# A hybrid decoder step: the second mixer's scores two steps sooner, its values turned later, and one function table loaded two steps later

## The chip, the cores and the metric

The kernel runs on one core of one Trainium2 chip. The metric is device time in microseconds (us). Engines: TensorE (PE) multiplies matrices, VectorE (DVE) and ScalarE (ACT) work on elements, GpSimd (POOL) gathers and moves, SyncE (SP) issues most transfers. All share one on-chip memory; matmul results go to a separate memory of a few buffers, which DVE and ACT read. Each engine runs its own instructions in the order in which the program gives them, and waits by semaphores for the others.

## What is computed

One layer of a decoder step for a prompt of 512 positions and 8 samples of one position each (520 columns in all), with a width of 2048. Two mixers work side by side on the same normed input: an mLSTM (matrix memory) and FoX (forgetting attention, 8 heads of 128). Their outputs are merged by gates, projected, and followed by a gated feed-forward part with a short convolution. The part of the reference that matters here is the prompt's attention and the merge:

```python
def block(args):
    qi, Fi, i = args
    qpos = i * Q_BLOCK + jnp.arange(Q_BLOCK)
    s = jnp.einsum('bqhd,bkhd->bhqk', qi, k).astype(jnp.float32) * scale
    s = s + (Fi.transpose(0, 2, 1)[..., :, None] - FkT[:, :, None, :])
    s = jnp.where(qpos[:, None] >= kpos[None, :], s, -jnp.inf)
    p = jax.nn.softmax(s, axis=-1).astype(v.dtype)
    return jnp.einsum('bhqk,bkhd->bqhd', p, v)
...
merged = jax.nn.sigmoid(ga) * (y_m @ w_proj_a) + jax.nn.sigmoid(gb) * (y_f @ w_proj_b)
x = x + g1 * (merged @ w_out)
```

Numbers are 32-bit floats. A product is made of three matmuls of rounded parts (high by high, high by low, low by high): ACT rounds a tile to its high part (`CAST`), DVE subtracts to get the low part (names that end in h and l).

## The kernel before

The kernel goes through the stages in order: conditioning and norms, the mLSTM, the input projections, the second mixer (FoX), the projections and merge, the output projection, the feed-forward part. In nearly all of them PE multiplies weights that stream in from memory, and the other engines prepare the next weights beside it.

**The second mixer.** Its attention alone would leave PE waiting for DVE and ACT, so it is woven into 16 half-products of the last 8 gates: 128 steps, each with six matmuls of the gate (`gate`, 260 columns each), 8 steps to a half. The loop is at the end of the listing below: behind a step's matmuls come the casts and loads of coming gate weights at fixed steps (`gate_cast` on ACT, `gate_low` on DVE, `gate_load` on SP), and then the pieces that `plan` holds for this step. `put(s, f, H)` enters a piece. Pieces of one step run in the order in which they were entered: all heads first, in order, then the samples' pieces (`s_*`). Each engine gets its instructions in just this order.

A head starts every `HP` = 13 steps at b = 1 + 13 * head. A head lasts 25 steps, so two are under way at any time. Its pieces:

- `f_load`, `f_roots`: SP loads q, k, the reciprocal roots of their norms (`rq`, `rk`, from `drr`) and V (from `dv`), all into tiles named `fi`. `f_norm`: two DVE instructions scale q and k.
- `f_forget`: a matmul spreads the head's forget sums (`nFb`), ACT copies them (`nfb`). `f_split`, `f_split_low`: high and low parts of q and k (`fqh`, `fkh` on ACT, `fql`, `fkl` on DVE).
- `f_values`: four transposes turn V (`vtp`), ACT makes its high part and copies the last block (`fvh`, `last`); `f_values_low`: `fvl` on DVE.
- `f_scores` i (0 to 3): block i of 128 queries against the (i+1)*128 keys up to it, into `fS`, with the mask added by one more matmul. `f_max` i: DVE adds the forget sums and finds the minimum in one custom instruction (`fs`, `sm`), ACT takes the exponential and its row sum. `f_scale` i: DVE divides (reciprocal, `fs<-fs,sm`).
- `f_turn` j (0 to 2): transposes the scaled rows of key block j, 4, 4 and 2 transposes, into `fPT`; block 3 is done beside block 1. ACT makes `fph`. `f_turn_low`: DVE makes `fpl` from `fPT` and `fph`.
- `f_attend` j: the product with V into `fy`; `f_result`: ACT copies it out.

Tiles of the matmul memory for these pieces (`nFb`, `vtp`, `fS`, `fPT`, `fy`, and the samples' `sS`, `sPT`, `sO`) come from one pool of four buffers, `pm`, handed out in turn: a new tile waits until the last reader of the tile four back is done with it.

Up to step 70 DVE also works off the sample scores (`s_scores`: a product `raw<-raw,qb` and a sum `sc<-raw`, two pieces for each i). Steps 71 to 81 hold the samples' softmax: `s_turn` (74, `sS`), `s_max`, `s_scale` (78, on DVE, tile `pp`), `s_weights` (79, transposes `sPT` of `pp`); then come the gathered values (`sO`).

**The output projection** runs in `run_pairs`: 7 products to a unit, and `late` gives functions to run ahead of the product of one step. At step 9 stands `log_exp`, which has ACT load the table that holds the logarithm and the exponential for the norm behind this stage. The products of a unit go to the tiles `x` and `y`; ACT copies `x` to `tg` before PE may write `x` again.

Of the kernel before, what the change touches and what calls it, by code (L numbers as in the profile page):

```python
# [18 lines left out]
P = 128  # L19
# [4 lines left out]
N = SEQ + NS  # L24
# [39 lines left out]
def tile_hybrid_step(ctx: ExitStack, tc: tile.TileContext, I, O):  # L64
    nc = tc.nc
    S, V, G, T, Y = nc.scalar, nc.vector, nc.gpsimd, nc.tensor, nc.sync
# [13 lines left out]
    def nm(s):  # L80
        uid[0] += 1
        return f"{s}{uid[0]}"
# [4 lines left out]
    def mconst(shape, name, dt=F32, tag=None):  # L87
        return cm.tile(shape, dt, tag=tag or name, name=name)

    def st(name, dt=F32):  # L90
        return sp.tile([P, 528], dt, tag="s", name=nm(name))
# [13 lines left out]
    def dram(shape, name):  # L105
        return dp.tile(shape, F32, tag=nm(name), name=nm(name))
# [68 lines left out]
    def on(f, *a):  # L175
        return lambda: f(*a)
# [550 lines left out]
    for i, (c0, n) in enumerate(phases):  # L727
        todo = {j: [] for j in range(NPRE)}

        def put(j, f, *a):  # L730
            todo[j].append(on(f, *a))
# [13 lines left out]
        if i + 1 < len(phases):  # L745
            a, b = range(c0 + n, c0 + 2 * n)
# [113 lines left out]
    for e in range(2):  # L860
        t = mconst([P, NS * NPG], f"idxf{e}")
# [355 lines left out]
    H = mheads = follows = None  # L1217
# [95 lines left out]
    dv = dram([FH, P, N], "dv")  # L1313
# [163 lines left out]
    dss, drr = dram([2, FH, N], "dss"), dram([2, FH, N], "drr")  # L1477
# [4 lines left out]
            Y.dma_start(t[:, :N], src)  # L1482

    def f_roots(H):
        H.rq, H.rk, H.v = st("fi"), st("fi"), st("fi")
        for t, src in ((H.rq, drr[0, H.i].partition_broadcast(P)), (H.rk, drr[1, H.i].partition_broadcast(P)),
                       (H.v, dv[H.i])):
            Y.dma_start(t[:, :N], src)

    def f_norm(H):  # L1490
        for t, w, r in ((H.q, qwc, H.rq), (H.k, nkw, H.rk)):
            V.scalar_tensor_tensor(t[:, :N], t[:, :N], w, r[:, :N], op0=ALU.mult, op1=ALU.mult)
        H.rq = H.rk = None
# [5 lines left out]
    for hh in range(FH):  # L1499
        H = Head()  # L1500
        H.i, H.p, H.pt, H.fs, H.sm, H.tp = hh, [], {}, {}, {}, {}
        heads.append(H)
    H = None
# [80 lines left out]
    for j in range(KC):  # L1584
# [11 lines left out]
        if j < NG:  # L1596
            t = sgs[j]
            V.tensor_tensor(z2(t), acc, z2(t), op=ALU.mult)
        else:
            t = pt("pao")  # L1600
# [11 lines left out]
    for n in (7, 4):  # L1612
        for i in range(8):
            t = st("hf", F32R)
# [4 lines left out]
    G, Y = (Ordered(tc, e) for e in (G, Y))  # L1619
# [70 lines left out]
    def f_max(H, i):  # L1690
        n = (i + 1) * P
        ps = H.fs.pop(i)
        s = st("fs")
        sm = tiny("sm")
        V.tensor_tensor_reduce(s[:, :n], ps[:, :n], H.nf[:, :n], -1.0, 3e38, ALU.add, ALU.min, sm[:, 0:1])
        S.activation(s[:, :n], s[:, :n], AF.Exp, bias=sm[:, 0:1], scale=-1.0, accum_out=sm[:, 1:2])
        H.p.append(s)
        H.sm[i] = sm
        if i == NB - 1:
            H.q = H.k = H.v = H.qr = H.kr = H.nf = None  # L1700

    def f_scale(H, i):
        n = (i + 1) * P
# [129 lines left out]
    for hh, H in enumerate(heads):  # L1833
        b = 1 + hh * HP
        if hh:
            put(max(1, b - 11), f_load, H)
            put(max(2, b - 8), f_roots, H)
            put(b, f_norm, H)
        put(b + 1, f_forget, H)
        put(b + 2, f_split, H)  # L1840
        put(b + 3, f_values, H)
        put(b + 4, f_split_low, H)
        put(b + 4, f_keys_out, H)
        put(b + 5, f_values_low, H)
        for s, i in ((8, 0), (9, 1), (11, 2), (12, 3)):
            put(b + s, f_scores, H, i)
            put(b + s + 1, f_max, H, i)
            put(b + s + 3, f_scale, H, i)
        for j in range(3):
            put(b + 17 + j, f_turn, H, j)  # L1850
            put(b + 18 + j, f_turn_low, H, j)
        for j in range(NB):
            put(b + min(21 + j, 23), f_attend, H, j)
        put(b + 24, f_result, H)
        put(max(100 + 3 * hh // 1, b + 25), y_split, hh)
        put(max(100 + 3 * hh // 1, b + 25) + 1, y_low, hh)
    put(3, s_offsets)
    put(5, s_keep)
    for i in range(4, 16):
        b = 8 + 11 * (i - 4) // 2  # L1860
# [12 lines left out]
    for n in range(8):  # L1873
        t = 83 + 5 * n
# [10 lines left out]
    H = None  # L1885
    mg = [None] * KC
# [37 lines left out]
    T, V, S, G, Y = nc.tensor, nc.vector, nc.scalar, nc.gpsimd, nc.sync  # L1924
# [34 lines left out]
    def m_parts(i, n):  # L1959
        if n == 5:  # L1960
            mX[5][i], mX[7][i] = hl_parts(hp, "hl", mg[i])
            return
        f = quarters(i)[3 if n == 6 else 2]
        t = (st if i == 7 else pt)("mf", F32R)
        hi, lo = mX[n][i] = parts_of(t)
        S.copy(hi, f)
        V.tensor_tensor(lo, f, hi.bitcast(F32), op=ALU.subtract)
        if i < 7:
            G.dma_start(dxf[i + 8 * (n == 4)][:, :N], t[:, :N])
# [182 lines left out]
    def load2(u, o, e):  # L2152
        raws[u, o, e] = wraw(I["w_fi"][u + o * KF][:, e * 1024:(e + 1) * 1024])
# [21 lines left out]
    for n in (6, 4):  # L2175
        for i in range(7):
            t = st("mf", F32R)
# [3 lines left out]
    def fetch_xa(cs):  # L2181
        for c in cs:
            xa[c] = st("xa")
            nc.sync.dma_start(xa[c][:, :N], dxa[c])
# [18 lines left out]
    def first_weights(o):  # L2203
# [3 lines left out]
    r2 = st("rr")  # L2207
    run_pairs(units, {
        0: lambda: (m_sums(7, 0), m_sums(7, 1)), 1: lambda: (m_parts(7, 5), m_sums(7, 2)),
        4: lambda: (m_parts(7, 4), mg.clear()), 9: log_exp, 50: lambda: fetch_xa(range(8)), 51: lambda: (load2(0, 0, 0), load2(0, 1, 0)), 53: tot_parts,  # L2210
        54: lambda: (first_weights(0), half_squares(1)), 55: lambda: (first_weights(1), half_norm(1))}, 0)
    mX = units = None

# [444 lines left out]
    for k in range(0, KC, 2):  # L2658
        t = 7 * (4 + 2 * k)
# [114 lines left out]
```

## Time and profile before

| | us |
|---|---|
| median of 3 runs | 2844.78 (2842.81 to 2845.59) |
| profiled execution | 2842.11 |
| its span | 2840.4 |
| second mixer in it | 1042.9 to 1202.8 |
| PE busy in the second mixer | 155.09 of 159.90 |
| DVE busy in the second mixer | 122.35 of 159.90 |
| ACT busy in the second mixer | 84.53 of 159.90 |

The granted clock of TensorE is 0.999 over the span, and 1.00 in every stretch of the second mixer. In a timeline a row has the start in us, the duration in us, the engine, the line, the operation, out<-in with the tiles' names, the shapes and the count of instructions merged into it; in square brackets stands the idle time of the engine just before, and what ended it. Rows of PE overlap, as matmuls are pipelined; from the start of one row to that of the next is the time that the engine needs. All pieces of the second mixer bear line 60, that of the helper that records them, so they are told apart by their tiles.

### The profile page before, as it was taken

The numbers are of one execution on the slowest core, as the hardware profiler recorded it, in microseconds if no ns is written. First come the engines' busy times: TensorE is split into PE (matmuls) and PEld (weight loads), VectorE is DVE, ScalarE is ACT, GpSimd is POOL, SyncE is SP. The second block draws the span as 40 slices with busy tenths as digits, with TensorE's granted clock in tenths as the row PEclk, the third lists the DMA queues.
The fourth block names the chain that finished last, engine by engine and source line by source line (L and its number), as shares of the span: only waits on it lengthen the run. The fifth ranks groups of instructions, "written<-read, shape, count | busy, mean of one in ns | idle before, by whom it ended". The sixth has DMA issues, their size and how long they took to land.

```text
span 2840.4 us, 57479 instructions
## 1 busy us (share of the span) xinstructions
PE 2808.3 (99%) x23270; PEld 2699.6 (95%) x23270; DVE 2172.9 (76%) x3300; ACT 1365.0 (48%) x2143; POOL 382.1 (13%) x659
## 2 busy tenths in 40 slices
PE   8999999999999999999999999999999999999999
PEld 6888998999999999899999999999999999999999
DVE  5986764576677789578888888787788888788787
ACT  4335553455555455445555444444444445444543
POOL 0001111201100132302211101011110101100100
PEclk9999999999999999999999999999999999999999
DMA  9946657855555578776672434444443346755753
GB/s 339 315 142 204 227 183 257 293 172 188 186 186 176 185 232 271 242 226 217 214 250 79 149 131 142 138 147 148 141 135 130 128 138 187 205 161 170 183 161 104
DMA packets 227842, 531.42 MB, mean 187 GB/s; under 512 B 30368, under 2 KB 83088, under 8 KB 227576
## 3 DMA queue, kind: packets, MB, share of 16 engines
q1 hardware_dynamic: 189600, 431.15, 46.8%
q0 software_dynamic: 37536, 96.38, 11.2%
q8 instruction: 182, 2.98, 0.4%
q14 instruction: 84, 0.69, 0.1%
q10 hardware_dynamic: 440, 0.23, 0.0%
HBM read 451.28 MB, written 72.92 MB: 185 GB/s over the span
## 4 chain that ended last, share of the span: by engine, by line
PE 90%; DVE 5%; DMA 2%; ACT 2%; issue 1%; SPq 0%; POOL 0%; ACTq 0%; DVEq 0%
PE x L60 35%; PE y L60 17%; PE z L60 9%; PE fo L60 4%; PE pa L213 3%; PE pb L213 3%; PE pre L60 3%; PE gate L60 2%; PE mo L213 2%; PE adp L60 2%; PE mv L213 2%; DMA ar<-in_w_ada 1%; DVE wl L60 1%; PE adp L409 1%; ACT wh L60 1%
## 5 line engine op out<-in xcount | busy, mean ns | idle before, releaser
L60 DVE TENSOR_TENSOR wl<-raw,wh 128x1024 fp32r<-128x1024 f32 (+1 forms) x696 | 838.7, 1206 | 358.4 <-ACT wh L60 355.7
L60 ACT CAST wh<-raw 128x1024 fp32r<-128x1024 f32 (+1 forms) x696 | 720.7, 1037 | 776.0 <-DVE raw L60 397.7
L60 PE MATMUL x<-bf,wh 128*128 128x260 f32 x2624 | 474.8, 282 | 0.0
L60 DVE TENSOR_TENSOR raw<-raw,raw 128x1024 f32<-128x1024 f32 x347 | 423.5, 1220 | 6.0
L60 PEld LDWEIGHTS x<-bf,wh 128*128 128x128 f32 x2624 | 403.2, 188 | 0.0
L60 PE MATMUL x<-bf,wl 128*128 128x260 f32 x1312 | 369.4, 282 | 0.0
L60 PEld LDWEIGHTS x<-bf,wl 128*128 128x128 f32 x1312 | 247.0, 188 | 0.0
L60 PE MATMUL y<-bf,wh 128*128 128x260 f32 x1312 | 239.1, 283 | 0.0
L60 PE MATMUL x<-hf,wh 128*128 128x260 f32 x1104 | 203.0, 284 | 0.0
L60 PEld LDWEIGHTS y<-bf,wh 128*128 128x128 f32 x1312 | 201.5, 188 | 0.0
L60 PE MATMUL x<-ff,wh 128*128 128x260 f32 x1024 | 186.1, 283 | 0.0
L60 PE MATMUL y<-bf,wl 128*128 128x260 f32 x656 | 185.1, 282 | 0.0
L60 PEld LDWEIGHTS x<-hf,wh 128*128 128x128 f32 x1104 | 169.7, 188 | 13.4 <-DVE tt L60 6.7
L60 PEld LDWEIGHTS x<-ff,wh 128*128 128x128 f32 x1024 | 157.5, 188 | 0.0
L60 PE MATMUL x<-hf,wl 128*128 128x260 f32 x552 | 155.7, 282 | 0.0
L168 DVE TENSOR_TENSOR wl<-raw,wh 128x1024 fp32r<-128x1024 f32 x68 | 83.1, 1223 | 88.7 <-ACT wh L167 87.4
L60 PE MATMUL x<-ff,wl 128*128 128x260 f32 x512 | 144.4, 282 | 0.0
L167 ACT CAST wh<-raw 128x1024 fp32r<-128x1024 f32 x68 | 71.3, 1049 | 135.1 <-DMA raw<-in_w_in 42.1
L60 PE MATMUL fo<-fe,wh 128*128 128x260 f32 x768 | 125.4, 284 | 1.0 <-DVE fo L60 0.7
L60 PEld LDWEIGHTS y<-bf,wl 128*128 128x128 f32 x656 | 123.3, 188 | 0.0
L60 PE MATMUL z<-bf,wh 128*128 128x260 f32 x656 | 119.1, 282 | 0.0
L60 PEld LDWEIGHTS fo<-fe,wh 128*128 128x128 f32 x768 | 105.8, 188 | 2.6 <-DVE fo L60 2.1
(640 smaller groups left out, 6984.5 us busy)
## 6 DMA issues: line engine op xcount, KB each, us to landing
raw<-in_w_fi SPq DMA_DIRECT2D x176, 512.0 KB
raw<-in_w_in SPq DMA_DIRECT2D x155, 512.0 KB
ar<-in_w_ada SPq DMA_DIRECT2D x192, 256.0 KB
raw<-in_w_ada SPq DMA_DIRECT2D x96, 512.0 KB
raw<-in_w_fo SPq DMA_DIRECT2D x64, 512.0 KB
raw<-in_w_out SPq DMA_DIRECT2D x32, 512.0 KB
raw<-in_w_fo SPq DMA_DIRECT2D x32, 384.0 KB
dff<-cc POOLq DMA_DIRECT2D x44, 260.0 KB
```

The lines of the kernel that those rows point to most:

```text
L60: return lambda *a, **k: self.tc.keep_in_program_order(getattr(self.eng, op)(*a, **k))
L167: S.copy(wh[:, :n], raw[:, :n])
L168: V.tensor_tensor(wl[:, :n], raw[:, :n], wh[:, :n].bitcast(F32), op=ALU.subtract)
L213: T.matmul(acc[:, z, :HN], a[:, o], b[:, z * HN:(z + 1) * HN], start=(k == 0 and i == 0), stop=(k == K - 1 and i == 2))
L409: ins = T.matmul(ps[32 * g:32 * g + 32, :], cs[:, k, :], w, start=first, stop=last, tile_position=(0, 32 * g))
```

## The change

The order of the pieces within a head changes, and one load is split off. With steps counted from the head's b:

| piece | before | after |
|---|---|---|
| load of V | -8 (with `rq`, `rk`) | 1 |
| `f_scores` 0 to 3 | 8, 9, 11, 12 | 6, 7, 9, 10 |
| `f_max`, `f_scale` | 1 and 3 after each | the same |
| `f_values`, `f_values_low` | 3, 5 | 11, 12 |
| `f_turn` 0 to 2, `f_turn_low` | 17 to 19, one later | 16 to 18, one later |
| `f_attend` 0 to 3 | 21, 22, 23, 23 | 20, 21, 22, 22 |
| `f_result` | 24 | 23 |

In the output projection `log_exp` moves from step 9 to step 11.

```diff
     def f_roots(H):
-        H.rq, H.rk, H.v = st("fi"), st("fi"), st("fi")
-        for t, src in ((H.rq, drr[0, H.i].partition_broadcast(P)), (H.rk, drr[1, H.i].partition_broadcast(P)),
-                       (H.v, dv[H.i])):
+        H.rq, H.rk = st("fi"), st("fi")
+        for t, src in ((H.rq, drr[0, H.i].partition_broadcast(P)), (H.rk, drr[1, H.i].partition_broadcast(P))):
             Y.dma_start(t[:, :N], src)
+
+    def f_load_values(H):
+        H.v = st("fi")
+        Y.dma_start(H.v[:, :N], dv[H.i])
...
         if i == NB - 1:
-            H.q = H.k = H.v = H.qr = H.kr = H.nf = None
+            H.q = H.k = H.qr = H.kr = H.nf = None
...
         put(b + 1, f_forget, H)
+        put(b + 1, f_load_values, H)
         put(b + 2, f_split, H)
-        put(b + 3, f_values, H)
         put(b + 4, f_split_low, H)
         put(b + 4, f_keys_out, H)
-        put(b + 5, f_values_low, H)
-        for s, i in ((8, 0), (9, 1), (11, 2), (12, 3)):
+        for s, i in ((6, 0), (7, 1), (9, 2), (10, 3)):
             put(b + s, f_scores, H, i)
             put(b + s + 1, f_max, H, i)
             put(b + s + 3, f_scale, H, i)
+        put(b + 11, f_values, H)
+        put(b + 12, f_values_low, H)
         for j in range(3):
-            put(b + 17 + j, f_turn, H, j)
-            put(b + 18 + j, f_turn_low, H, j)
+            put(b + 16 + j, f_turn, H, j)
+            put(b + 17 + j, f_turn_low, H, j)
         for j in range(NB):
-            put(b + min(21 + j, 23), f_attend, H, j)
-        put(b + 24, f_result, H)
+            put(b + min(20 + j, 22), f_attend, H, j)
+        put(b + 23, f_result, H)
...
-        4: lambda: (m_parts(7, 4), mg.clear()), 9: log_exp, 50: ...
+        4: lambda: (m_parts(7, 4), mg.clear()), 11: log_exp, 50: ...
```

What stands on the engines now, at three places. First DVE, from the scaling of head 0's block 2 to the second `fpl` of head 0, while head 1 begins (`fi_12675` and `fi_12676` are head 1's q and k). Before:

```order
L60 TENSOR_SCALAR fs_12807<-fs_12807,sm_12808 128x384
L60 TENSOR_REDUCE sc<-raw_12658 128x2x4
L60 RECIPROCAL sm_12829<-sm_12829 128x1
L60 TENSOR_SCALAR fs_12828<-fs_12828,sm_12829 128x512
L60 TENSOR_TENSOR fql_12857<-fi_12675,fqh_12856 128x512
L60 TENSOR_TENSOR fkl_12860<-fi_12676,fkh_12859 128x512
L60 TENSOR_TENSOR fpl_12899<-fPT_12893,fph_12898 128x512
L60 TENSOR_TENSOR fvl_12880<-vtp_12874,fvh_12879 128x384
L60 TENSOR_TENSOR raw_12741<-raw_12741,qb_12739 128x1024
L60 TENSOR_TENSOR wl_12891<-raw_12667,wh_12890 128x1024
L60 TENSOR_TENSOR fpl_12919<-fPT_12913,fph_12918 128x384
```

The same stretch of DVE now:

```order
L60 TENSOR_SCALAR fs_12781<-fs_12781,sm_12782 128x384
L60 TENSOR_TENSOR fvl_12807<-vtp_12801,fvh_12806 128x384
L60 TENSOR_TENSOR raw_12658<-raw_12658,qb_12656 128x1024
L60 RECIPROCAL sm_12798<-sm_12798 128x1
L60 TENSOR_SCALAR fs_12797<-fs_12797,sm_12798 128x512
L60 SCALAR_TENSOR_TENSOR fi_12675<-fi_12675,qwc,fi_12708 128x520
L60 SCALAR_TENSOR_TENSOR fi_12676<-fi_12676,nkw,fi_12709 128x520
L60 TENSOR_REDUCE sc<-raw_12658 128x2x4
L60 TENSOR_TENSOR fpl_12880<-fPT_12874,fph_12879 128x512
L60 TENSOR_TENSOR fql_12857<-fi_12675,fqh_12856 128x512
L60 TENSOR_TENSOR fkl_12860<-fi_12676,fkh_12859 128x512
L60 TENSOR_TENSOR fpl_12898<-fPT_12892,fph_12897 128x384
```

The scaling of block 3 (128x512) has moved ahead of head 1's norm (before, the norm stood ahead of this stretch), the first `fpl` ahead of `fql` and `fkl`, and the second directly behind them; `fvl` is now that of head 0 itself.

Second PE, head 0's products and head 1's first scores, after the last `fPT` of head 0:

```order
L60 MATMUL fS_12938<-mask_f,identb 128x128
L60 MATMUL gate_12849<-hh_882,wh_12647 128x260 x2
L60 MATMUL gate_12849<-hl_883,wh_12647 128x260 x2
L60 MATMUL gate_12849<-hh_882,wl_12648 128x260 x2
L60 MATMUL fy_12947<-fph_12879,fvh_12806 128x512
L60 MATMUL fy_12947<-fpl_12880,fvh_12806 128x512
L60 MATMUL fy_12947<-fph_12879,fvl_12807 128x512
L60 MATMUL fS_12955<-fkh_12859,fqh_12856 128x256
L60 MATMUL fS_12955<-fkl_12860,fqh_12856 128x256
L60 MATMUL fS_12955<-fkh_12859,fql_12857 128x256
```

Scores 0 of head 1 now stand one step ahead of head 0's first product `fy`, and scores 1 in the same step behind it; before, scores 0 stood behind `fy` in its step, and scores 1 one step later, behind the second product.

Third ACT in the output projection (`wh` are casts of weights, `tg` is the copy of `x`). Before:

```order
L60 CAST wh_16281<-raw_16032 128x1024
L60 ACT_TABLE_LOAD
L60 COPY tg_16314<-x_16212 128x260
L60 CAST wh_16316<-raw_16132 128x1024
L60 CAST wh_16349<-raw_16034 128x1024
L60 CAST wh_16386<-raw_16254 128x1024
```

And now:

```order
L60 CAST wh_16281<-raw_16032 128x1024
L60 COPY tg_16313<-x_16212 128x260
L60 CAST wh_16315<-raw_16132 128x1024
L60 CAST wh_16348<-raw_16034 128x1024
L60 ACT_TABLE_LOAD
L60 CAST wh_16386<-raw_16254 128x1024
```

The load has moved behind the copy and two casts.

More of the change, by code (lines that the diff above doesn't have):

```diff
@@ L2209, in tile_hybrid_step @@
         0: lambda: (m_sums(7, 0), m_sums(7, 1)), 1: lambda: (m_parts(7, 5), m_sums(7, 2)),
-        4: lambda: (m_parts(7, 4), mg.clear()), 9: log_exp, 50: lambda: fetch_xa(range(8)), 51: lambda: (load2(0, 0, 0), load2(0, 1, 0)), 53: tot_parts,
+        4: lambda: (m_parts(7, 4), mg.clear()), 11: log_exp, 50: lambda: fetch_xa(range(8)), 51: lambda: (load2(0, 0, 0), load2(0, 1, 0)), 53: tot_parts,
         54: lambda: (first_weights(0), half_squares(1)), 55: lambda: (first_weights(1), half_norm(1))}, 0)
```

## The prediction

> **What bounds the kernel now.** I read the page first (busy time by engine, the chain that ended last), then the table by stretch of the second mixer, then TensorE's waits there, then the timelines of TensorE, VectorE and ScalarE at the places of those waits.
>
> ```profile
> PE 2808.3 (99%) x23270; PEld 2699.6 (95%) x23270; DVE 2172.9 (76%) x3300; ACT 1365.0 (48%) x2143; POOL 382.1 (13%) x659
> PE 90%; DVE 5%; DMA 2%; ACT 2%; issue 1%; SPq 0%; POOL 0%; ACTq 0%; DVEq 0%
> ```
>
> TensorE (PE) is busy for 99% of the span and carries 90% of the chain. The change removes no instruction on any engine; it only moves some. So it can win nothing but time in which PE stands still, in the two places it touches. The first is the second mixer, 1042.9 to 1202.8 us. Its table by stretch has the columns us, PE, PEld, DVE, ACT, POOL, clock, DMA share, GB/s:
>
> ```profile
> 1070.00:1090.00 20.00, 20.00 (x157) 18.78 (x157) 19.53 (x44) 11.51 (x28) 8.11 (x8) 1.00 0.98 324
> 1090.00:1110.00 20.00, 19.60 (x154) 18.38 (x152) 19.16 (x39) 11.72 (x27) 9.07 (x9) 1.00 0.89 306
> 1110.00:1130.00 20.00, 19.28 (x150) 18.15 (x150) 19.42 (x38) 12.17 (x28) 0.95 (x1) 1.00 0.81 242
> 1130.00:1150.00 20.00, 18.73 (x138) 15.96 (x138) 12.78 (x36) 8.51 (x21) 7.67 (x9) 1.00 0.66 201
> ```
>
> Up to 1130 VectorE (DVE) is as full as PE: it idles 60.00 - 19.53 - 19.16 - 19.42 = 1.89 us in 60. After 1130 the sample scores are done and DVE has room. PE's waits from 1020 to 1215, as us in total, times, longest:
>
> ```profile
> PE fPT L60 <- DVE fs L60: 2.0, 2, 1.1
> PE fS L60 <- issue: 1.8, 1, 1.8
> PE fS L60 <- DVE fpl L60: 0.6, 1, 0.6
> PE fy L60 <- DVE fpl L60: 0.2, 1, 0.2
> PE fy L60 <- issue: 0.2, 1, 0.2
> ```
>
> That is 4.8 us in six waits: all that the first part of the change could remove.
>
> **The waits for scaled rows, and why I expect them back.** f_turn of block 0 needs f_scale of block 3. The longer of the two waits, at head 0, in PE's timeline (the other, at head 3, is the 0.9 that is left of the 2.0):
>
> ```profile
> 1063.48 0.33 PE L60 MATMUL fPT<-ident,fs 128*128 128x128 f32 x1 [1.07 <-DVE fs L60]
> ```
>
> f_scale of block 3 stood two steps ahead of f_turn; it now stands three ahead, and on DVE in front of the next head's norm instead of behind it. So these two waits go (-1.07 and -0.9). But DVE gets no less to do, and another wait is ready. The four matmul buffers are handed out in turn. Before, the buffer of f_turn block 1 went to f_scores block 1 three steps on; now it does two steps on, and it is free only when DVE has made `fpl` of block 1 from it. On DVE `fpl` of block 0 now also stands ahead of `fql` and `fkl`. Head 5, the last one in the full stretch, in the timelines of PE and DVE:
>
> ```profile
> 1124.43 0.60 PE L60 MATMUL vtp<-ident,fi 128*128 128x128 f32 x4
> 1124.79 0.49 PE L60 MATMUL gate<-hh,wh 128*128 128x260 f32 x2
> ...
> 1127.67 0.68 DVE L60 TENSOR_TENSOR fkl<-fi,fkh 128x512 fp32r<-128x512 f32 x1
> 1128.28 1.21 DVE L60 TENSOR_REDUCE sc<-raw 128x8 f32<-128x1024 f32 x1
> ...
> 1129.06 0.40 PE L60 MATMUL gate<-hh,wh 128*128 128x260 f32 x2
> ...
> 1129.40 0.68 DVE L60 TENSOR_TENSOR fpl<-fPT,fph 128x512 fp32r<-128x512 f32 x1
> ...
> 1130.14 0.50 PE L60 MATMUL fy<-fph,fvh 128*128 128x512 f32 x1 [0.20 <-DVE fpl L60]
> ```
>
> On DVE: `fkl` ended its turn at 1128.28. With `fpl` of block 0 ahead of it (0.60: below, the next row starts that much after one of this shape) that is 1128.88; the reduction takes 1.12 (1128.28 to 1129.40), then `fpl` of block 1 takes 0.48 (0.56 in the row at 1150.08 below, less the 0.08 by which neighbouring rows overlap). It ends at 1130.48.
>
> ```profile
> 1077.24 0.60 PE L60 MATMUL vtp<-ident,fi 128*128 128x128 f32 x4
> ...
> 1080.31 0.68 DVE L60 TENSOR_TENSOR fkl<-fi,fkh 128x512 fp32r<-128x512 f32 x1
> 1080.91 0.68 DVE L60 TENSOR_TENSOR fpl<-fPT,fph 128x512 fp32r<-128x512 f32 x1
> ```
>
> On PE: the pieces of a step follow its gate matmuls, which take 0.72 (1147.35 to 1148.07 below). From the place of `vtp` in the old order (1124.43) the new one runs: turn 0 (0.36, four transposes like `vtp`, 1124.43 to 1124.79), turn 1 (0.36), turn 2 (half of that, 0.18), scores 0 (0.36, 1150.68 to 1151.04), attend 0 (0.71: a gate's six matmuls of 260 columns take 0.72, so 0.24 for one of 512, three times) and four gate groups (2.88). That is 4.85, so scores 1 would be reached at 1129.28 and waits 1.20 us. For head 2 the same sum gives 1082.09 on PE against 1080.91 + 0.60 + 0.48 = 1081.99 on DVE: no wait, but on a clock that already holds the 1.07 us of head 0. So what head 0 gains is used up by head 2.
>
> At head 5 the balance is: scores 1 takes 0.41 (by columns) and ends at 1130.89. The old order stood at 1129.06 with 0.71 + 0.36 + 0.41 - 0.36 = 1.12 less work done (attend 0, scores 0 and 1, against `vtp`) and 0.20 of waiting ahead, so it reaches the same amount at 1130.38. The new order is 0.5 late there if DVE's rows stay where they are. But PE's earlier progress lets DVE use some of its 1.89 us of idle time; I take half, 0.95. **This stretch: -0.4 us**, with bounds of -1.4 (all idle time used) and +1.5 (none used, and ScalarE's cast `fph` late by about one more row of 1 us).
>
> **A wait that the change adds.** For head 5 f_values now stands at step 77 and f_values_low at 78, on DVE ahead of the sample rows' scale, which the transposes `sPT` at step 79 need. Durations, from rows of the same kind:
>
> ```profile
> 1106.33 0.68 DVE L60 CUSTOM_DVE_ANT_0 fs<-fS,nfb 128x512 f32<-128x512 f32 x1
> ...
> 1138.92 0.72 ACT L60 ACTIVATE fs<-fs,sm 128x512 f32<-128x512 f32 x1 [1.02 <-DVE sm L60]
> ...
> 1143.58 0.48 ACT L60 CAST fvh<-vtp 128x384 fp32r<-128x384 f32 x1
> ...
> 1104.26 0.15 DVE L60 RECIPROCAL sm<-sm 128x1 f32<-128x1 f32 x1
> 1104.45 0.36 DVE L60 TENSOR_SCALAR fs<-fs,sm 128x256 f32<-128x256 f32 x1
> ```
>
> From the end of scores 3 the chain is the maximum 0.68, exponential 0.72, `fvh` 0.48, `fvl` 0.56 (the shape at 1150.08), reciprocal 0.15, scale 0.36: 2.95 us. PE has three gate groups and `vtp` in that time: 2.52. With a little for the hand-overs, **+0.5 us** (0 if the rows overlap by 0.08 each as above; +0.9 with a gap of 0.1 at five hand-overs). Behind the waiting `sPT` stand only gate matmuls.
>
> The other moves cost nothing. V's load stood with the two loads of `drr` and now goes to SP's queue nine steps later, ten steps ahead of its use. The loads of `drr`, on the same queue, stand eight steps ahead of their use, and none of the six waits is for a DMA. The low parts of q and k are needed three steps after they are made instead of five; DVE makes them ahead of `fpl` of block 1, so scores 1 waits for its buffer later than for them.
>
> **The stall after step 87.** The largest wait, 1.76 us, and the 0.6 after it:
>
> ```profile
> 1145.62 0.49 PE L60 MATMUL gate<-hh,wh 128*128 128x260 f32 x2
> ...
> 1147.35 0.41 PE L60 MATMUL gate<-hh,wh 128*128 128x260 f32 x2
> ...
> 1148.07 0.39 PE L60 MATMUL fy<-fph,fvh 128*128 128x512 f32 x1
> ...
> 1149.40 0.48 ACT L60 CAST fph<-fPT 128x384 fp32r<-128x384 f32 x1 [4.57 <-remote]
> ...
> 1150.08 0.56 DVE L60 TENSOR_TENSOR fpl<-fPT,fph 128x384 fp32r<-128x384 f32 x1 [4.06 <-remote]
> ...
> 1150.68 0.49 PE L60 MATMUL fS<-fi,fi 128*128 128x128 f32 x2 [1.76 <-issue]
> ...
> 1151.04 0.48 PE L60 MATMUL gate<-hh,wh 128*128 128x260 f32 x2
> ```
>
> ScalarE starts the cast of turn 1 only at 1149.40, though PE had left its transposes for the gate by 1145.62; nothing that the trace names holds it. Then `fpl`, then the buffer, then `fS` are late. With scores 0 now in another buffer this wait goes if the cast is in time; if it is late again, scores 1 meets it. The rows can't decide that, so the bounds are -2.4 (1.76 and 0.6) and 0, and I take the middle, **-1.2 us**.
>
> **The table.** In the output projection's first pair:
>
> ```profile
> 1326.23 1.28 ACT L60 ACT_TABLE_LOAD   x1
> 1327.53 0.38 ACT L60 COPY tg<-x 128x260 f32<-128x260 f32 x1
> ...
> 1331.03 1.05 ACT L60 CAST wh<-raw 128x1024 fp32r<-128x1024 f32 x1 [1.23 <-PE x L60]
> ...
> 1326.87 0.28 PE L60 MATMUL y<-mf,wl 128*128 128x260 f32 x1
> 1327.95 0.51 PE L60 MATMUL x<-mf,wh 128*128 128x260 f32 x2 [0.81 <-ACT tg L60]
> ...
> 1326.25 1.23 DVE L60 TENSOR_TENSOR wl<-raw,wh 128x1024 fp32r<-128x1024 f32 x1 [1.17 <-ACT wh L60]
> ```
>
> PE waits 0.81 us for the copy `tg`, which stands behind the load. Moved two steps on, the load falls into ScalarE's idle 1.23 us ahead of 1331.03 and overhangs by 0.05. PE then starts 0.81 us sooner, but its second product needs `wl`, which ends at 1327.48, where PE would be at about 1327.3. So **-0.6 us** (bounds -0.81, and +0.3 if the load delays the next cast and its `wl`).
>
> [...]
>
> **Sum:** -0.4 + 0.5 - 1.2 - 0.6 = -1.7 us, against the profiled execution's 2842.11 us (span 2840.4). The median of the runs shown, 2844.78, lies 2.67 above it, and the runs spread over 2.8. I carry the sum to the median: 2843.1 us. Bounds added: -1.4 + 0 - 2.4 - 0.8 = -4.6 and +1.5 + 0.9 + 0 + 0.3 = +2.7.
>
> **Rivals.** *All waits go.* 4.8 + 0.81 us, and some 0.15 for each of the seven restarts (from 1326.87 + 0.12, where PE would have gone on, to 1327.95 it is 0.96 with a wait of 0.81): 6.7 us, so 2838.1. For it: each of the six waits hangs on a distance in steps that grows, or on a buffer that changes. Against it: DVE at 97% up to 1130, and the new neighbours above. *Waits only change places:* every microsecond gained comes back at scores 1 and `sPT`, the cast is late again, and the table is the only gain, less the 0.5: about 2844.7. *Slower, by the buffer of turn 1.* Scores 1 now follows turn 1 by 0.72 + 0.18 + 0.72 + 0.36 + 0.72 + 0.71 = 3.41 us on PE. A cast as late as that at 1149.40 (3.78 us after 1145.62) plus 0.48 and 0.56 is 4.82, so each such head costs 1.4 us, eight cost 11.2: 2856. It decides the sign from five heads on (+7.0). For it: the cast has been late once, with no cause to be seen. Against it: in the other heads it follows within the time of its neighbours. [...]
>
> **How the numbers follow.** Forecast 0.55; waits change places 0.25; all go 0.08; slower by the buffer 0.08; the drain 0.04. A measurement of this kernel can tell about 0.2%, 5.7 us, from no change. The forecast, the changed places and the drain lie inside that: 0.84. All go lies just beyond it: faster 0.08; slower 0.08. The forecast's own bounds are 2840.2 to 2847.5; the range reaches to the first rival's 2838 on one side, and to 2848, short of the slow rival, on the other.
>
> **What would show it.** Right: no `fPT` waits for `fs`; `fS` of 256 columns waits for `fpl` in heads 2 to 5; `sPT` waits for `pp` by about half a microsecond; DVE stays above 95% up to the end of the sample scores; `tg` follows the cast directly and the next cast starts near 1331. Wrong: DVE idles where it was full and scores 1 doesn't wait (then the gain is real), scores 1 waits past 1130 too, or `vtp` waits for V's DMA.

## The result, and the profile after

The changed kernel is slower: 2860.61 us median of 6 runs (2858.15 to 2861.91), against 2842.79 for the kernel before (6 runs, 2841.88 to 2845.59). The ratio is 1.0059, interval 1.0046 to 1.0072. That is +17.8 us where -1.7 was forecast; the range ended at 2848. Which chip these runs had is not known; it is called the first chip below.

Busy time, and the chain of waits of the changed kernel. The chain's shares sum to 47%, so it was followed back over less than half of the span, and what bounds the second mixer is read from the stretches instead:

```profile
PE 2816.4 (99%) x23270; PEld 2705.0 (95%) x23270; DVE 2174.5 (76%) x3300; ACT 1364.8 (48%) x2143; POOL 382.3 (13%) x659
PE 44%; DVE 2%; ACT 1%; issue 0%; DMA 0%; POOL 0%; SPq 0%; ACTq 0%; DVEq 0%
```

The work is the same: as many instructions on each engine, and nearly the same busy time. The stretches of the second mixer (columns as before):

```profile
1070.00:1090.00 20.00, 18.68 (x141) 17.01 (x140) 18.61 (x40) 10.72 (x26) 7.33 (x6) 1.00 0.96 280
1090.00:1110.00 20.00, 18.71 (x143) 17.14 (x142) 17.93 (x39) 10.65 (x25) 7.00 (x8) 1.00 0.88 289
1110.00:1130.00 20.00, 16.90 (x128) 15.29 (x127) 15.55 (x33) 8.09 (x22) 3.85 (x4) 1.00 0.74 249
1130.00:1150.00 20.00, 17.50 (x135) 15.90 (x134) 17.21 (x40) 9.55 (x23) 0.53 (x1) 1.00 0.62 173
1150.00:1170.00 20.00, 16.02 (x108) 12.94 (x106) 6.93 (x19) 7.91 (x18) 8.76 (x9) 0.91 0.84 290
1190.00:1215.00 25.00, 21.57 (x157) 17.16 (x158) 9.66 (x20) 9.49 (x20) 7.10 (x7) 0.93 0.47 157
```

VectorE, full before up to 1130 (19.53, 19.16 and 19.42 of 20), now stands idle for 1.39, 2.07 and 4.45 us in the same stretches, and TensorE with it. PE's waits from 1020 to 1230 (us in total, times, longest):

```profile
PE fS L60 <- DVE fpl L60: 8.8, 5, 3.7
PE sOT L60 <- ACT ob L60: 3.4, 1, 3.4
PE fPT L60 <- DVE fs L60: 1.9, 2, 1.3
PE sPT L60 <- DVE sm L60: 0.7, 1, 0.7
PE fy L60 <- DVE fpl L60: 0.6, 1, 0.6
PE fS L60 <- DVE fkl L60: 0.6, 1, 0.6
PE fy L60 <- issue: 0.3, 1, 0.3
```

Before, the waits summed up to 4.8 us; now it is 16.3. The largest part, 8.8 us in five, is scores 1 waiting for `fpl`: 5.1 us in heads 2 to 5, the wait that the prediction priced for head 5, and 3.67 us in head 6.

What a step costs is read better from the start of its gate matmuls than from the idle times, since idle time counts only from the modelled end of a matmul (before the change PE stands idle for 0.81 us for the copy `tg`, where the starts of its matmuls give 0.96). Step n of a run starts so much later than in the first trace of the kernel before, both counted from step 0. Each row is one trace; the names are those of the runs below, and "late" at the end of a row marks traces with late results, explained under the jumps:

```
us behind the first trace      step 29   55     81     107    127
changed kernel                  -0.1     3.4    8.4    11.4   16.6   late
changed kernel, f1              -0.2     3.3    6.6     4.0    4.1
changed kernel, e12             -0.2     3.3    5.1     2.8    2.8
values late alone, e1           -0.2     1.0    1.8     0.3    0.4
values early, rest moved, e2    -0.8     1.1    1.5    -0.4   -0.4
scores 1 a step later, f2       -0.2     1.9    3.6     1.0    1.1
fvl a step later, f3            -1.2     0.8    0.9    -1.6   -1.6
fvl a step later, g2            -1.1     0.8    4.2     7.2   10.9   late
both a step later, g3            1.0     1.7    1.2     0.7    5.0   late
kernel before again, g1          1.6     2.2    2.4     4.7    4.7   late
```

The first trace of the kernel before, the zero of this table, has late results itself, with its stall of 1.76 us behind step 87. So the fall of 1.4 to 2.6 us behind step 81 in the rows without "late" is in the main time that the first trace lost, not time that they won.

Two things lie on top of each other: a loss of 5 to 7 us from step 29 to step 81, that is in heads 2 to 5, in every run of the changed kernel (e12 and f1 show it alone), and jumps of 3 to 5 us behind steps 55, 81 and 107 in the changed kernel's first trace, with late results.

**The loss in heads 2 to 5.** VectorE in the changed kernel, head 1's values and what follows up to head 2's second `fpl`:

```profile
1076.14 0.42 DVE L60 TENSOR_SCALAR fs<-fs,sm 128x384 f32<-128x384 f32 x1
1077.44 0.56 DVE L60 TENSOR_TENSOR fvl<-vtp,fvh 128x384 fp32r<-128x384 f32 x1 [0.88 <-ACT last L60]
...
1083.25 0.68 DVE L60 TENSOR_TENSOR fpl<-fPT,fph 128x512 fp32r<-128x512 f32 x1
1083.85 0.68 DVE L60 TENSOR_TENSOR fql<-fi,fqh 128x512 fp32r<-128x512 f32 x1
1084.45 0.68 DVE L60 TENSOR_TENSOR fkl<-fi,fkh 128x512 fp32r<-128x512 f32 x1
1085.05 0.55 DVE L60 TENSOR_TENSOR fpl<-fPT,fph 128x384 fp32r<-128x384 f32 x1
```

```profile
1085.65 0.38 PE L60 MATMUL fS<-fkh,fqh 128*128 128x256 f32 x1 [0.71 <-DVE fpl L60]
```

The second fence is PE's row for scores 1, which start as `fpl` ends. The new thing is the 0.88 us at 1077.44. Behind the last exponential of a head ScalarE turns the values (`fvh`, `last`), and VectorE reaches `fvl` before that is done. Its rows keep the program's order, so the sample work, the scaling and the norm behind `fvl` stand too (they start at 1077.92, 1079.23 and 1079.64). In another run of the changed kernel, f1 below, ScalarE at the same place:

```profile
1092.73 0.72 ACT L60 ACTIVATE fs<-fs,sm 128x512 f32<-128x512 f32 x1 [1.03 <-DVE sm L60]
...
1093.45 0.46 ACT L60 CAST fvh<-vtp 128x384 fp32r<-128x384 f32 x1
1093.81 0.26 ACT L60 COPY last<-vtp 128x128 f32<-128x128 f32 x1
```

The exponential waits for VectorE's maximum, `fvh` for the exponential, and VectorE, one scaling later, for `fvh` (by its row until `last`, the copy behind it, is done).

**The jumps.** At step 86 and step 111 of the changed kernel, PE, ScalarE and VectorE in order of time:

```profile
1155.16 0.38 PE L60 MATMUL fPT<-ident,fs 128*128 128x128 f32 x2
1161.38 0.37 ACT L60 CAST fph<-fPT 128x256 fp32r<-128x256 f32 x1 [6.79 <-remote]
1161.79 0.42 DVE L60 TENSOR_TENSOR fpl<-fPT,fph 128x256 fp32r<-128x256 f32 x1 [4.21 <-issue]
1162.27 0.39 PE L60 MATMUL fS<-fkh,fqh 128*128 128x256 f32 x1 [3.67 <-DVE fpl L60]
...
1201.46 0.48 ACT L60 CAST fph<-fPT 128x384 fp32r<-128x384 f32 x1 [4.63 <-remote]
1201.99 0.60 ACT L60 COPY ob<-sO 128x512 f32<-128x512 f32 x1
1202.65 0.66 PE L60 MATMUL sOT<-ident,ob 128*128 128x128 f32 x4 [3.43 <-ACT ob L60]
```

The transposes are recorded at 1155.16 to 1155.54, and ScalarE, with nothing else to do, casts them 5.8 us later; nearly 4 us the second time. It is what the prediction saw once, at 1149.40 of the kernel before. The jump behind step 55 starts so too: `fvh` at 1111.83 after [2.12 <-PE nFb], and VectorE's `fvl` at 1112.51 after 1.98 us. I call these **late results**. Behind these two stalls PE's clock falls; the changed kernel in stretches of 3 us:

```profile
1160.00:1163.00 3.00, 0.73 (x5) 0.64 (x5) 0.68 (x3) 0.87 (x3) 0.54 (x1) 0.93 1.03 412
1163.00:1166.00 3.00, 3.00 (x15) 3.00 (x14) 1.32 (x6) 0.60 (x3) 0.00 (x0) 0.50 1.03 400
1166.00:1169.00 3.00, 3.00 (x24) 1.94 (x24) 0.56 (x2) 1.25 (x4) 0.01 (x1) 1.00 0.88 344
...
1203.00:1206.00 3.00, 3.00 (x15) 2.71 (x14) 2.66 (x8) 2.44 (x4) 0.00 (x0) 0.59 0.07 26
```

Behind 3.67 us of idle time the granted clock was 0.50 for about 3 us (15 matmuls in 3 us, against 24 in the next 3), so that such a stall costs more than its own length. Behind the 1.76 us of the kernel before it stayed at 1.00. Other runs show that the length of one wait doesn't decide it: the clock was 0.50 from 1136.2 to 1139.6 us in f1 behind a wait of 1.83 us (0.91 in the mean from 1130 to 1150), and from 1082.5 to 1085.9 us in e4 behind one of 1.88 (0.91 from 1070 to 1090), while in e12 the same wait of 1.83 us and in e6 one of 2.89 us left it at 1.00. What makes the difference between these cases is not shown. The slower clock is also why f1 has lost 6.6 us by step 81 and e12, the same kernel, 5.1: up to step 68 both are 3.0 us behind, and 3.4 us at 0.50 cost about 1.7 us, by an estimate from f1's clock.

**The table** did what was forecast. ScalarE in the changed kernel:

```profile
1343.71 0.37 ACT L60 COPY tg<-x 128x260 f32<-128x260 f32 x1
1343.98 2.00 ACT L60 CAST wh<-raw 128x1024 fp32r<-128x1024 f32 x2
1346.00 1.28 ACT L60 ACT_TABLE_LOAD   x1
1347.95 1.05 ACT L60 CAST wh<-raw 128x1024 fp32r<-128x1024 f32 x1 [0.67 <-PE x L60]
```

```profile
1344.55 0.28 PE L60 MATMUL y<-mf,wl 128*128 128x260 f32 x1
1344.67 0.40 PE L60 MATMUL x<-mf,wh 128*128 128x260 f32 x2
1345.12 0.39 PE L60 MATMUL x<-mf,wl 128*128 128x260 f32 x1
```

PE (second fence) goes on to `x` without a wait, and loses 0.21 us at `wl` (1345.12 instead of 1344.67 + 0.24). Before it was 0.96, so the table gives 0.75 us back.

### The profile page after: what moved, and what is told of

Its sections match the earlier page's. It is cut to its first block, busy times and chain, and to the rows that moved or that the text cites. A ratio compares the mean times of both kernels' runs of the same rounds, so it can differ in the third digit from the quotient of the medians.

```text
span 2858.7 us, 57497 instructions
## 1 busy us (share of the span) xinstructions
PE 2816.4 (99%) x23270; PEld 2705.0 (95%) x23270; DVE 2174.5 (76%) x3300; ACT 1364.8 (48%) x2143; POOL 382.3 (13%) x659
## 5 line engine op out<-in xcount | busy, mean ns | idle before, releaser
L60 DVE TENSOR_TENSOR raw<-raw,raw 128x1024 f32<-128x1024 f32 x347 | 423.4, 1220 | 5.9
```

Of the source, the lines that this page charges most:

```text
L60: return lambda *a, **k: self.tc.keep_in_program_order(getattr(self.eng, op)(*a, **k))
```

## The experiments

Four theories. **A**: scores 1 stand two steps behind the `fpl` whose buffer they take (before, three), too few while VectorE is full. **B**: the late values make VectorE stand at `fvl`. **C**: both in a loop: scores 1 wait for `fpl`, so the later scores and the values come late, so VectorE stands at `fvl`, so the next `fpl` is late; it opens wherever it is cut. **D**: late results of TensorE on the chip at hand. The runs come in five groups, each on one chip of its own, beside the kernel before. In what follows the ratio is to the kernel before on that chip.

### First group: each half of the change alone, and more room

e1, on the kernel before:

```diff
+        put(b + 1, f_load_values, H)
...
-        put(b + 3, f_values, H)
...
-        put(b + 5, f_values_low, H)
...
+        put(b + 11, f_values, H)
+        put(b + 12, f_values_low, H)
```

V's load is split off `f_roots` as in the change.

> The kernel before with V's load, its turning and its low part moved to steps 1, 11 and 12; scores, turns and products stay where they were. Theory A (the change is slow because scores 1 now follow the turn whose buffer they take by two to three steps, while VectorE is full): scores 1 still stand three to four steps behind that turn, so no new waits, 2841 to 2845 us. Theory B (it is slow because the late values make VectorE stand at `fvl` until ScalarE is through with the last exponential, 0.9 to 2.0 us a head): most of the loss is here, 2849 to 2857 us.

e2, on the changed kernel: the same three pieces put back to -8, 3 and 5.

> The changed kernel with V's load, turning and low part put back to their old steps (load 8 steps ahead, 3 and 5). Theory A: scores 0 to 3 and the turns stay as close together as in the changed kernel; the first product `fy` now takes the buffer of turn 1 and scores 0 that of turn 0, two to three steps on, so PE waits in each head as before, 2853 to 2860 us. Theory B: the stand at `fvl` is gone, 2843 to 2849 us.

e3, on the changed kernel:

```diff
-        for s, i in ((6, 0), (7, 1), (9, 2), (10, 3)):
+        for s, i in ((6, 0), (8, 1), (9, 2), (10, 3)):
```

> The changed kernel with scores 1 (and its maximum and scaling) one step later, 8 for 7; all buffers are handed on in the same order. Theory A: a step gives PE 0.7 to 1.2 us of other work ahead of the wait, in eight heads, so a good part of the 17.8 us comes back, 2848 to 2854 us. Theory B: VectorE stands at `fvl` as before and its rows set the end, so no more than a microsecond or two, 2858 to 2862 us.

e4, on the changed kernel: `((7, 0), (8, 1), (10, 2), (11, 3))` in the same line.

> The changed kernel with the scores moved by one step instead of two (7, 8, 10, 11). Scores 1 take the buffer of turn 1 three to four steps after it, and scores 0 that of turn 0 four steps after it. Theory A: the waits of scores 1 go almost wholly, 2842 to 2849 us. Theory B: the values stand where they stood in the changed kernel, and VectorE waits for them as much, 2856 to 2861 us.

Measured, with the kernel before at 2840.27: e1 2843.46 (1.0008, 0.9998 to 1.0017), e2 2842.43 (1.0007, 0.9997 to 1.0017), e3 2844.19 (1.0012, 1.0002 to 1.0022), e4 2846.06 (1.002, 1.001 to 1.003). So neither half alone costs more than 0.17%, the end of the intervals, and neither makes the 17.8 us on this chip. This shows less than I took it to show, for two reasons. The changed kernel itself was not run here, and it turned out later to lose only 5.5 to 6.3 us on such a chip: beside that, the 3.2 us of e1 and the 2.2 of e2 are a good half and a third. And e1 doesn't make the stand that B is about: with the scores at their old steps, `fvh` goes ahead of the exponentials of blocks 2 and 3 (1089.90, then 1090.43 and 1092.08), and `fvl` waits for 2.0 us in all, at most 0.6 at a time. So e1 doesn't rule B out; e2 does speak against A alone, as its waits for `fpl` sum up to 4.2 us, not far below the 5.3 of the changed kernel in f1, at a third of the price. Of e4 A expected that nearly all waits go, and its time was no better than that of the scores two steps sooner with one of them held back. Its trace gives the reason: the waits of `fS` are gone, and those of `fPT` for `fs` are there instead, since scaling of block 3 again stands only two steps ahead of turn 0:

```profile
PE fPT L60 <- DVE fs L60: 5.0, 4, 1.9
```

### Second group: the other cut, part of the heads, and VectorE with less to do

e5, on the changed kernel, so that `fvl` stands behind the scaling of block 3:

```diff
-        put(b + 12, f_values_low, H)
+        put(b + 13, f_values_low, H)
```

> The changed kernel with only f_values_low one step later (13 for 12), so that on VectorE `fvl` stands behind the scaling of block 3 and no longer makes it and everything behind it stand until ScalarE has turned the values. Scores 1 still take the buffer of turn 1 two steps on. Theory A alone (the two steps between turn 1 and scores 1 are too few for a full VectorE): the waits of scores 1 stay, 2855 to 2861 us. Theory C (a loop: scores 1 wait for `fpl`, so scores 3 and the values are late, so VectorE stands at `fvl`, so the next `fpl` is late; it opens wherever it is cut): most comes back, 2842 to 2850 us.

e6, on the changed kernel: `(7 + (hh < 6), 1)` for `(7, 1)`.

> The changed kernel with scores 1 a step later (8 for 7) in heads 0 to 5 alone, where VectorE also works off the sample scores. Theories A and C: the 8 us lost up to step 79 come back; for the second half of the loss, after the first product of the gathered values at step 83, they say that heads 6 and 7 have waits of their own, so 2849 to 2854 us. Rival (the late loss follows from the early one): all comes back, 2843 to 2847 us.

e7 and e8, on the changed kernel and on the kernel before, leave out 24 pieces of the sample scores, so their output is not that of the reference:

```diff
+    V.memset(sc, 0.0)
...
-        put(b, s_scores, i, 0)
-        put(b + 2, s_scores, i, 1)
+        put(b + 2, W.k.pop, i)
```

> The changed kernel without the scores of 12 of the 16 pairs of sample and half of heads (24 pieces on VectorE, some 1.2 us each, up to step 70 are left out; their scores stay zero). If it takes a full VectorE for the change to lose time, scores 1 wait no more up to step 73, and what stays is the loss behind step 83: 6 to 9 us more than the next kernel. If the order alone loses it, however full VectorE is: 15 to 18 us more than the next kernel.

> The kernel before without the same 24 pieces, for comparison with the run above. PE's waits up to step 70 there sum up to some 2.5 us, so 2838 to 2843 us.

Measured, with the kernel before at 2842.70: e5 2849.20 (1.0022, 1.0012 to 1.0032), e6 2852.40 (1.0031, 1.0021 to 1.0042), e7 2847.92 (1.002, 1.001 to 1.0029), e8 2843.27 (1.0004, 0.9994 to 1.0013). e7 is 4.7 us above e8. With VectorE busy for 11.48, 11.39 and 12.18 of 20 us from 1050 to 1110, scores 1 wait for `fpl` only once up to step 73, 0.6 us, so these waits do take a full VectorE. The time doesn't show as much: in e7 PE also stands in the gate's own matmuls at step 38, for 2.3 us in four waits (e8: 0.6 in one), which is no part of any theory; from step 29 to 42, around these waits, e7 loses 3.0 us on e8.

```profile
PE gate L60 <- issue: 2.3, 4, 1.0
PE fS L60 <- DVE fpl L60: 0.6, 1, 0.6
```

The changed kernel itself wasn't run in this group, so how much of its loss here each edit takes away is not shown. PE's waits of e6: those of scores 1 for `fpl` are gone in heads 0 to 5, but the products `fy` wait for `fpl` in their place, and a wait of 2.9 us in head 6 remains.

```profile
PE fy L60 <- DVE fpl L60: 3.0, 4, 1.2
PE fS L60 <- issue: 2.9, 1, 2.9
```

### Third group: the second half, and the changed kernel once more

e9, on the changed kernel: `(7 + (hh >= 6), 1)` for `(7, 1)`. e10, on the changed kernel:

```diff
-        t = 83 + 5 * n
+        t = 87 if n == 0 else 83 + 5 * n
```

> The changed kernel with scores 1 a step later in heads 6 and 7 alone. If the losses of the two halves are separate, the 8.4 us up to step 79 stay and the 4 to 6 us at step 86 go: 2850 to 2856 us. If the loss behind step 79 is only a consequence of the earlier delay, it stays: 2857 to 2862 us.

> The changed kernel with the first product of the gathered values (step 83, `sO`) at step 87, behind scores 1 of head 6; the buffers from there on are handed on in another order (scores 1 of head 6 take turn 1's of head 5). In the trace ScalarE gets the transposes that follow `sO` late (the cast at 1161.38 us). If `sO` ahead of the turns is what makes the stall at step 86, it goes, and 3 to 6 us come back: 2853 to 2858 us. If not, scores 1 wait there as before, 2858 to 2862 us.

e11, on the kernel before, with the table at 11: `((7, 0), (8, 1), (10, 2), (11, 3))`. e12 is the changed kernel itself.

> The kernel before with the scores one step sooner (7, 8, 10, 11) and nothing else moved but the table (step 11): scaling of block 3 stands three steps ahead of turn 0, scores 1 three steps behind turn 1, values early. If both distances count, the waits of `fPT` for `fs` (2.0 us) go and none of scores 1 comes: 1 to 4 us faster than before. If VectorE sets the end here anyway, no difference beyond 0.1%.

> The changed kernel once more, for the trace alone: waits of scores 1 of 0.7 to 1.8 us in heads 2 to 5 and of 3 to 4 us in head 6 if they belong to the order; the wait of 3.4 us at step 111 too, if it does.

Measured, with the kernel before at 2840.74: e9 2845.85 (1.0019, 1.001 to 1.0028), e10 2848.12 (1.0027, 1.0018 to 1.0036), e11 2842.91 (1.0008, 0.9999 to 1.0017), e12 2846.23 in its one run. The last was the surprise: the changed kernel was 5.5 us above the kernel before here, not 17.8, and the waits expected in head 6 and at step 111 are not in its trace. So these numbers must not be set against the 2860.61. Beside the one run of e12, e9 gives nothing, and e10 nothing either: without a stall at step 86 there is nothing to win there. Whether `sO` ahead of the turns brings the late results on stays open, as this chip shows none. e11 isn't faster than the kernel before: its trace has no wait of `fPT` for `fs`, but scores 1, now two steps behind `fpl`, wait for it for 3.2 us in four waits. There the waits only changed places.

How late ScalarE casts TensorE's results (`fph`, `fvh`, `nfb`) was worked out for each trace: from the later of the end of the last transpose (or matmul) and the end of ScalarE's operation before, to the start of the cast, summed over the 40 casts. Beside it the number of semaphore events that the trace holds in the second mixer (from 1040 to 1220 us):

```
trace                      casts late by, us   over 2 us late at     semaphore events
before, first trace            10.8            1112, 1149, 1152      2230
changed kernel                 16.4            1112, 1116, 1161, 1201 2080
e1, e2, e3, e4                 0.4 to 1.3      none                  3088 to 3112
e5                             12.9            1112, 1155, 1191      2182
e6, e7, e8                     6.0 to 7.3      one or two each       2102 to 2262
e9, e10, e11, e12              0.4 to 1.2      none                  3033 to 3112
f1, f2, f3                     0.4 to 0.6      none                  3039 to 3121
g1, g2, g3                     10.7 to 17.3    one to four each      2114 to 2237
```

All traces of one group are alike. The groups are of two kinds: those with late results, whose traces also lack about a third of the semaphore events of this stretch, and those with neither.

### Fourth group: the changed kernel and the two cuts on one chip

f1 is the changed kernel, f2 the edit of e3, f3 the edit of e5.

> The changed kernel against the kernel before, timed anew. If its loss of 17.8 us belongs to the order alone: 2857 to 2863 us on this chip too. If some 12 us of it come from results of TensorE that reach ScalarE 2 to 6 us late, which the traces of one pair of chips show and those of another pair don't: 2857 to 2863 us where the trace shows them, 2844 to 2849 us where it doesn't.

> The changed kernel with scores 1 one step later, on the same chip as the run before. If the two steps between turn 1 and scores 1 are what costs the time, it lies within 0.15% of the kernel before, with late results (scores 1 then have one step, 0.7 to 1.2 us, more room in each head) or without; if late results alone make the loss, it is as slow as the changed kernel where they show.

> The changed kernel with f_values_low one step later, on the same chip. Where no late results show: if the stand at `fvl` feeds the loop, 2841 to 2844 us, below the changed kernel; if it doesn't, as the changed kernel. Where they show: 2845 to 2852 us as before.

Measured, with the kernel before at 2840.39: f1 2846.72 (1.0021, 1.0013 to 1.003), f2 2843.91 (1.0011, 1.0002 to 1.002), f3 2840.61 (0.9997, 0.9988 to 1.0007). No trace of this group shows late results. So the order alone loses 6.3 us, 0.21%; scores 1 a step later give a little under half of it back, and one piece on VectorE moved by one step all of it. PE's waits of f1:

```profile
PE fS L60 <- DVE fpl L60: 4.4, 5, 1.8
PE fy L60 <- DVE fpl L60: 0.9, 2, 0.6
PE sPT L60 <- DVE sm L60: 0.7, 1, 0.7
PE fPT L60 <- DVE fs L60: 0.6, 1, 0.6
```

and of f3:

```profile
PE fS L60 <- DVE fpl L60: 3.0, 4, 0.9
PE fy L60 <- DVE fpl L60: 0.3, 1, 0.3
```

On VectorE the waits of `fvl` for ScalarE sum up to this in f1, and f3 has no such row:

```profile
DVE fvl L60 <- ACT last L60: 4.4, 5, 0.9
```

One such place in f1 (first row), and the same piece in f3 (second row):

```profile
1094.11 0.56 DVE L60 TENSOR_TENSOR fvl<-vtp,fvh 128x384 fp32r<-128x384 f32 x1 [0.88 <-ACT last L60]
...
1092.41 0.55 DVE L60 TENSOR_TENSOR fvl<-vtp,fvh 128x384 fp32r<-128x384 f32 x1
```

That the stand at `fvl` is a necessary part of the loss is shown by f3. Theory C expects more, and the traces have it: with the stand cut out, the waits of scores 1 get shorter (1.8 to 0.9 us at most), and those of `sPT` and `fPT` go, though nothing was done to them; and f2 wins time although `fvl` waits as long as before (4.9 us). B alone doesn't explain f2, nor A alone f3. The loop itself is argued: a plain sum of two losses (3.2 us in e1 and 2.2 in e2, together 5.4) would come near f1's 6.3 too, but would leave f3 some 2 us above the kernel before, where 0.2 was measured (-3.4 to +2.0 by the interval).

### Fifth group: both cuts, and the kernel before again

g1 is the kernel before, g2 the edit of e5, g3 the edits of e3 and e5 together.

> The kernel before once more, for its trace. If the late results are a matter of the chip, a trace without them shows no stall of 1.8 us behind step 87 and the waits of `fPT` for `fs` alone (2 to 4 us), and the second mixer takes 2 to 4 us less than in the first trace; otherwise both stalls are there.

> The changed kernel with f_values_low one step later, timed with more rounds. Where no late results show it should be level with the kernel before as in the last call (0.9988 to 1.0007); where they show, 2 to 9 us slower.

> The changed kernel with both cuts: f_values_low at 13 and scores 1 at 8. If each cut gives back a part of its own, this one is faster than either and than the kernel before, 2836 to 2840 us where no late results show. If VectorE is the bound once the loop is open, it is level with f_values_low alone, 2839 to 2842 us.

Measured, with the kernel before at 2845.36: g2 2852.12 (1.0025, 1.0016 to 1.0034), g3 2853.14 (1.0028, 1.0019 to 1.0037), g1 2848.53 in its one run. This group has late results, and with them the cut at `fvl` doesn't reach the kernel before: it is 6.8 us above it, as e5 was 6.5. As the changed kernel itself was run on neither of these two chips, what the cut wins there is not measured. g1 shows the stall of the kernel before behind step 87 again (`PE fS <- issue`, 3.3 us), and the sOT wait of step 111 is there in g2, as in the first trace of the changed kernel:

```profile
PE fS L60 <- DVE fpl L60: 6.7, 5, 3.0
PE sOT L60 <- ACT ob L60: 3.4, 1, 3.4
```

No trace here shows the kernel before without late results, and so g3's question, whether both cuts give more than one, stays open. No variant of the kernel is faster than the kernel before; f3, e1, e2 and e11 can't be told from it.

## Why the prediction was wrong

**The waits for scaled rows go, -1.07 and -0.9:** half right. That at head 0 is gone; that at head 3 is gone in f1, but still 1.26 us on the first chip, behind a late result; and one of 0.62 us comes in at head 1 in both, where the scaling itself is late.

**This stretch: -0.4 us** is the step that failed. Up to step 81 the changed kernel lost 5.1 to 8.4 us, and the bounds of this term ended at +1.5. The mechanism, scores 1 waiting for `fpl` in turn 1's buffer, was the one named, and heads 2 to 5 have it (0.71, 0.71, 1.84 and 1.83 us on the first chip; priced at 1.20 for head 5 and at nothing for head 2; its "three steps on" and "two" are counted from `fpl`, from the turn itself they are four and three). What failed is the premise under the balance, that VectorE's rows stay where they are and that it even gains idle time to use. I had counted its work and not its order. `fvl` had moved behind the last exponential and `fvh`, 0.88 us in a head even where TensorE's results come in time, and everything behind it moved with it. I had worked out that very chain for `sPT` at head 5 and called the values' move free otherwise ("The other moves cost nothing"). f3 shows it: `fvl` one step later takes the whole loss away where no late results are. A sign that the prediction had set for being wrong came: scores 1 wait past 1130 too (1139.32 and 1162.27). One that it had set for being right failed: VectorE's busy share falls under 95% while the sample scores last (17.93 of 20 us).

**A wait that the change adds, +0.5 us** at `sPT`: right, 0.67 us on the first chip and 0.7 in f1.

**The other moves cost nothing:** right for V's load, no wait for its transfer is in any trace; wrong for the values' low part.

**The stall after step 87, -1.2 us:** wrong in sign on the first chip. The stall didn't go with the buffer. Behind the samples' tiles the buffers are handed on in another order, and scores 1 of head 6 take that of turn 2, which I had not followed that far; with the cast 5.8 us late the wait was 3.67 us, and a second one of 3.43 us came at step 111 through `ob`, which stands behind a late cast on ScalarE. In the groups without late results neither stall is there. Why the casts come late in some groups is not known.

**The table, -0.6 us:** right, 0.75.

**The rivals.** "Slower, by the buffer of turn 1", at a chance of 0.08, has the right sign and nearly the size, 2856 us against 2860.61, but the size is luck. It was taken as a case of late casts in five heads or more; yet 6.3 us of the loss need no late cast at all, and the other 11.5 (17.8 less 6.3, from two sets of runs) came with late casts at three places rather than in each head. That the late casts cause these 11.5 us is argued from the one trace, not tested. "Changed places" gave the right view, that what is won comes back at scores 1, without what makes it grow. A drain beside the table's load, which has a chance of 0.04 in the prediction and a part in its 0.84, shows in no run: before, the copy `tg` starts 0.02 us after the load's end; now TensorE waits 0.21 us there, and the cast behind the load starts 0.67 us after it, when TensorE has done `x`.

## What to carry to other kernels

Where two engines are both full, a wait that is moved is not a wait that is removed (in e4 5.0 us of `fPT` stood where those of `fS` had gone): ask of each instruction that is moved on the second engine what it waits for there, and what stands behind it in order. An operation that needs a result of a third engine (here `fvl` behind ScalarE's last cast) belongs behind work that is ready, not ahead of it: one step made 6.1 us (f1 against f3). And time a change of a few tenths of a per cent on more than one chip before its cause is sought: here it cost 0.2% in two sets of runs and 0.6% in one.

## What the runs showed of the hardware

In three of the six sets of runs (the first chip, the second and the fifth group) ScalarE started on results of TensorE 2 to 6 us after the recorded end of the transposes, with nothing else to do: between 1109 and 1117 us in four traces, at 1189 to 1201 us in four, and at 1148 to 1161 us, shortly after the first products of the gathered values, in all nine traces that show late results. The 11 traces of the three other groups show none over 2 us. Late results go along with 2080 to 2262 semaphore events from 1040 to 1220 us instead of 3033 to 3121, and with a kernel before that takes 2842.7 to 2845.4 us instead of 2840.3 to 2840.7.

What is late is TensorE's signal as the trace has it. In the first trace of the changed kernel the next four updates of its semaphore behind the first `sO` stand 0.54, 1.99, 3.42 and 6.97 us behind the recorded end of `sO`, and the late cast starts 0.02 us after the last of them; in f1 all four come within 0.12 us. Busy transfer engines alone don't bring it on: in e12, without late results, the DMA share is 1.02 to 1.03 from 1155 to 1167 us, in the changed kernel's first trace 0.94 and 1.00 from 1155 to 1161 us. Whether the data are late or the signal alone, whether recording causes the delay and the loss of events, and whether the chip or the occasion decides, as no chip had two groups, was not tried and stays open.
